# Last token group of a hybrid decoder layer: the eight samples as eight more columns of the first feed-forward product, in halves of 256 tokens

## The chip, the cores and the metric

One core of a Trainium2 chip runs the whole kernel. Its engines work side by side, each through its own list of instructions in order: TensorE (PE in the profile, with its weight loads as PEld), VectorE (DVE), ScalarE (ACT), GpSimd (POOL), and SyncE (SP), which here issues nearly all DMAs. Products land in PSUM, which holds eight banks of 512 float32 words per partition; all else lives in SBUF. The metric is the device time of one execution in microseconds (us), the median of several.

## The reference

One layer of a decoder, applied to a prompt of 2048 tokens and to eight single-token samples with the same weights. Only the second half of the layer matters here:

```python
mixed = concatenate([o_gdn, o_att]) @ w_out           # 1024 -> 1024
x = x + ga1 * mixed
h2 = _rmsnorm(x, g_norm2) * (1.0 + sc2) + sh2         # per-sequence sc2, sh2
gate, up = split(h2 @ w_ffn_in, 2)                    # 1024 -> 2 x 2816
x = x + ga2 * ((silu(gate) * up) @ w_ffn_out)         # 2816 -> 1024
y = _rmsnorm(x, g_final)
```

The prompt and each sample have scales (`sc2`, `ga1` and so on) of their own; the weights are shared.

## The kernel before

The prompt is worked in four groups of 512 tokens (`GT`). `ffn(g)` computes the lines above for group `g`. The first three groups run between attention work; the last one (`samp` is true) also carries the eight samples and runs alone, after everything else is done.

**Split products.** Each float32 product is made of three matmuls in a faster format: both operands are split in a high part (a cast on ACT) and a low part (a subtraction on DVE or POOL), and `mm3` (L199 to L201) issues high x high, high x low and low x high. Every matmul loads its stationary operand of 128 columns and then streams up to 512 columns.

**Weights.** `weights` (L164) brings a tile of 128 x 512 by DMA, casts it on ACT (L182) and subtracts on DVE (L183). In the last group six split tiles are in flight (tags `wi`, and `kT` with `V`), so the cast of a tile waits until TensorE is done with the tile six before it.

**First product.** The 2816 hidden columns go in eleven pairs of 256. A weight tile of a pair holds 256 gate columns and 256 up columns: four stationary blocks `j` = 0 to 3 of 128 (0 and 1 gate, 2 and 3 up). For each of eight `k` (1024 = 8 x 128) and each `j`, `mm3` streams the 512 tokens (`hh`, `hl`) into one PSUM bank; four banks of tag `d` hold the results. Behind a pair, ACT takes tanh of a gate bank (L2115), DVE forms silu(gate) x up (L2116, L2118), ACT casts (L2121) and POOL subtracts (L2122).

**Samples.** Their eight rows are too few to be worth a stream, so they are the stationary operand: high parts in columns 0 to 7 and low parts in columns 32 to 39 of one block of 40, against which the weight tile streams as 512 columns, once for its high and once for its low part (`mm_s`, L215 and L216, into a bank of tag `g`). `fold` adds the two row groups (L222, L223), `gate` forms the activation in rows (L2065 to L2067), and `turned` transposes it back to columns (L2072) for the second product. These side jobs wait in a list (`side`) that `tick` empties behind each weight tile.

**Second product.** After two pairs (or the last one alone), four (two) row blocks of `w_ffn_out` are applied in two halves of 512 output columns; here tokens are stationary, one bank per 128 tokens. Results are scaled by a row (L1876, DVE) and added into `xt` (L1877, POOL). In the last half of all, the tokens' blocks come one by one (`kept`), and `finish` closes each: squares on ACT, `rnorm` (sum on DVE L471, power -0.5 on POOL L472), scaling in two halves on ACT and DVE, and the DMA out.

**Last norm ahead of the feed-forward.** In the second half of `w_out`, the last two `k` of eight are kept back and applied token block by token block; `shut(t)` adds, squares, norms and scales block `t` (L1966 or L1968). Then `hidden_T` transposes all four blocks for one `k` (L500, four transposes), and makes `hh` and `hl` of it (L502 to L504). Six of the eight `k` are transposed while the first pair runs. The samples' own norm and transposes (`turn`, L2023 to L2031) run as side jobs in the first pair.

The order of instructions on an engine follows the order of the code and the Tile framework's scheduling; in this last group nothing else competes.

## Time and profile before

| | |
|---|---|
| median of 3 runs | 3539.82 us (3529.56 to 3540.5) |
| the profiled execution | 3521.95 us, span of its instructions 3520.2 us |
| busy in the span | TensorE 94%, weight loads 73%, VectorE 60%, ScalarE 42%, GpSimd 17% |
| granted TensorE clock, mean | 0.977 |
| chain that ended last | TensorE 72%, DMA 9%, VectorE 8%, waits without a cause shown 4%, ScalarE 4% |
| first matmul of the last group's first pair | at 3061.97 us |
| last matmul of the kernel's second product | at 3501.23 us |

Busy time counts a matmul until its modelled end, so that streams overlap in it: where TensorE is full, what one matmul costs is the distance from its start to the next one's start. Times within a view are us from the span's start. In a row of the timeline stand start, duration, engine, line, operation, output and inputs with their sizes and, in brackets, how long the engine was idle before it and what ended that.

### The profile page before, as it was taken

How to read it: one execution, taken by the hardware profiler on the slowest of the kernel's cores; microseconds unless marked ns; L12 is line 12 of the kernel's file. 1: busy time of each engine (PE TensorE's matmuls, PEld its weight loads, DVE VectorE, ACT ScalarE, POOL GpSimd, SP SyncE). 2: the span in 40 equal slices, each digit the busy share in tenths (PEclk: the TensorE clock that was granted, in tenths of full speed). 3: DMA queues.
4: the chain of work that ended last, by engine and by line, in shares of the span. 5: the costliest groups of instructions: out<-in, count | busy, mean ns of one | idle time of the engine just before them, and what ended most of it. 6: DMA issues, size and time to landing. Idle time of an engine off the chain costs nothing.

```text
span 3520.2 us, 60159 instructions
## 1 busy us (share of the span) xinstructions
PE 3323.2 (94%) x21994; PEld 2584.3 (73%) x21994; DVE 2121.4 (60%) x4502; ACT 1472.9 (42%) x2855; POOL 584.5 (17%) x539
## 2 busy tenths in 40 slices
PE   7899999999998899999989999999899999999997
PEld 5677777777776777777766777777777777677775
DVE  4656545646844767666767656567666654555445
ACT  4333322423433333454565545455554633323223
POOL 1001000100000132212210122222012212222223
PEclk8999999999999999999999999999999999999999
DMA  8765764775785254555463454336433333422221
GB/s 285 270 204 167 246 210 146 225 242 177 239 284 186 92 177 115 157 165 163 148 200 109 121 164 151 90 111 209 131 96 97 101 110 112 162 82 81 81 81 56
DMA packets 421013, 549.60 MB, mean 156 GB/s; under 512 B 50020, under 2 KB 287817, under 8 KB 420698
## 3 DMA queue, kind: packets, MB, share of 16 engines
q1 hardware_dynamic: 420690, 545.62, 49.1%
q8 instruction: 175, 2.87, 0.3%
q14 instruction: 132, 1.08, 0.1%
q10 hardware_dynamic: 16, 0.03, 0.0%
HBM read 441.78 MB, written 122.70 MB: 160 GB/s over the span
## 4 chain that ended last, share of the span: by engine, by line
PE 72%; DMA 9%; DVE 8%; issue 4%; ACT 4%; SPq 2%; POOL 1%; ACTq 0%; DVEq 0%; POOLq 0%
PE d L199 17%; PE d L201 16%; PE d L200 16%; PE s L1740 3%; PE g L1802 3%; PE s L1785 3%; DMA wi<-kept 2%; DMA wr<-in_w_ffn_in_dram 1%; PE g L1814 1%; DVE wi L183 1%; ACT bias L1609 1%; PE g L215 1%; PE g L216 1%; DMA wr<-in_w_out_dram 1%; ACT wi L182 1%
## 5 line engine op out<-in xcount | busy, mean ns | idle before, releaser
L199 PE MATMUL d<-hh,wi 128*128 128x512 f32 x1616 | 687.9, 426 | 21.1 <-DVE th L2116 7.6
L200 PE MATMUL d<-hl,wi 128*128 128x512 f32 x1616 | 639.1, 395 | 3.2 <-DVE hl L504 3.0
L201 PE MATMUL d<-hh,wi 128*128 128x512 f32 x1616 | 638.6, 395 | 0.5 <-DVE wi L183 0.5
L183 DVE TENSOR_TENSOR wi<-wr,wi 128x512 fp32r<-128x512 f32 x525 | 392.0, 747 | 408.1 <-ACT wi L182 403.8
L182 ACT CAST wi<-wr 128x512 fp32r<-128x512 f32 x525 | 324.4, 619 | 693.6 <-PE d L201 397.9
L199 PEld LDWEIGHTS d<-hh,wi 128*128 128x128 f32 x1616 | 308.2, 191 | 104.6 <-issue 11.7
L200 PEld LDWEIGHTS d<-hl,wi 128*128 128x128 f32 x1616 | 308.2, 191 | 74.3 <-issue 10.1
L201 PEld LDWEIGHTS d<-hh,wi 128*128 128x128 f32 x1616 | 307.1, 190 | 69.1 <-DVE wi L183 1.1
L199 PE MATMUL d<-wi,hh 128*128 128x512 f32 x736 | 316.3, 430 | 19.9 <-DMA wi<-kept 10.6
L200 PE MATMUL d<-wi,hh 128*128 128x512 f32 x736 | 291.0, 395 | 1.0 <-DVE wi L183 1.0
L201 PE MATMUL d<-wi,hl 128*128 128x512 f32 x736 | 291.2, 396 | 0.0
L199 PE MATMUL d<-wi,ah 128*128 128x512 f32 x616 | 267.6, 434 | 11.5 <-ACT ah L2121 5.4
L2122 POOL TENSOR_TENSOR al<-ca,ah 128x512 fp32r<-128x512 f32 x88 | 120.3, 1378 | 806.6 <-ACT ah L2121 772.8
L201 PE MATMUL d<-wi,al 128*128 128x512 f32 x616 | 246.1, 400 | 2.4 <-POOL al L2122 2.4
L200 PE MATMUL d<-wi,ah 128*128 128x512 f32 x616 | 245.3, 398 | 0.0
L1749 DVE SCALAR_TENSOR_TENSOR sc<-rl,iw,sc 128x512 f32<-128x512 f32 (+3 forms) x224 | 173.3, 774 | 74.6 <-ACT rl L1742 68.8
L1877 POOL TENSOR_TENSOR xt<-xt,tm 128x512 f32<-128x512 f32 x96 | 136.3, 1434 | 439.1 <-DVE tm L1876 331.1
L1742 ACT ACTIVATE rl<-s 128x512 f32<-128x512 f32 (+3 forms) x288 | 151.3, 542 | 137.6 <-PE s L1740 130.1
L199 PEld LDWEIGHTS d<-wi,hh 128*128 128x128 f32 x736 | 139.8, 190 | 63.5 <-DMA wi<-kept 10.5
L1609 ACT ACTIVATE bias<-sc,sv 128x640 bf16<-128x640 f32 (+11 forms) x120 | 169.8, 1415 | 26.4 <-DVE sv L1611 14.1
L1740 PE MATMUL s<-ik,iqT 128*128 128x512 f32 (+3 forms) x576 | 171.7, 392 | 3.1 <-DVE st L1786 1.6
L201 PEld LDWEIGHTS d<-wi,hl 128*128 128x128 f32 x736 | 139.7, 190 | 31.8 <-issue 0.3
(570 smaller groups left out, 5937.8 us busy)
## 6 DMA issues: line engine op xcount, KB each, us to landing
wi<-kept SPq DMA_DIRECT2D x168, 512.0 KB
wr<-in_w_ffn_in_dram SPq DMA_DIRECT2D x584, 128.0 KB
wr<-in_w_ffn_out_dram SPq DMA_DIRECT2D x148, 256.0 KB
kept<-wi SPq DMA_DIRECT2D x56, 512.0 KB
row<-in_w_ada_dram SPq DMA_DIRECT2D x32, 512.0 KB
wr<-in_w_in_dram SPq DMA_DIRECT2D x56, 256.0 KB
xt<-in_x_prompt_dram SPq DMA_DIRECT2D x7, 2048.0 KB
kT<-kT_d SPq DMA_DIRECT2D x54, 256.0 KB
```

The costliest lines, as they stand in the source:

```text
L182: nc.scalar.copy(hi, wr)
L183: nc.vector.tensor_tensor(lo, wr, hi.bitcast(F32), op=OP.subtract)
L199: self.o(nc.tensor.matmul(out, wh, xh, start=start, stop=False, **kw))
L200: self.o(nc.tensor.matmul(out, wh, xl, start=False, stop=False, **kw))
L201: self.o(nc.tensor.matmul(out, wl, xh, start=False, stop=stop, **kw))
L1609: nc.scalar.activation(c, s, AF.Sign, bias=t, accum_out=cnt)
L1740: self.o(nc.tensor.matmul(ps[:, :w], iq[:, h, :].bitcast(F32R), B["ikT"][c * 2 + a][:, :w].bitcast(F32R), start=a == 0, stop=a == 1))
L1742: nc.scalar.activation(r[:, :w], ps[:, :w], AF.Relu)
L1749: nc.vector.scalar_tensor_tensor(s, r[:, :w], iw, s, op0=OP.mult, op1=OP.add)
L1785: self.o(nc.tensor.matmul(ps[:, :w], qT[:, h, :], kT[:, :w], start=True, stop=True))
L1877: (nc.vector if soon else nc.gpsimd).tensor_tensor(xt, xt, tm, op=OP.add)
L2122: nc.gpsimd.tensor_tensor(al[b], a, ah[b].bitcast(F32), op=OP.subtract)
```

## The change

It touches the last group alone (but for helper lines, so that line numbers grow by 2 ahead of `ffn` and by 14 to 40 in it).

- The eight samples are no longer a stationary operand of the first product. Their normed and transposed values stand as columns 256 to 263 of the second half of `hh` and `hl`, and stream with it. A PSUM bank holds 512 columns, not 520, so the tokens go in halves: 256 of the first half (from tiles of tag `big`, into two banks of tag `s`, which hold gate and up side by side) and 264 of the second (into the four banks of tag `d`). Blocks go in the order 0, 2, 1, 3. `mm_s` and its `fold`, `gate` and `turned` are gone from the first product; in the second they stay.
- The activation behind a pair is made half by half, in twice as many instructions of half the size; two small POOL copies per block put the samples' columns into the stationary block of the second product.
- In the first pair, `k` 0 to 3 run for the first half of the tokens, then for the second half, then `k` 4 to 7 likewise; transposes (`half_T`) come two blocks at a time.
- Three `k` of `w_out` are kept back, not two, and the samples' part of `w_out` is finished ahead of the token blocks. The samples' norm (`turn`) is called behind the second block; it scales on ACT, its transposes stand in the first pair behind `k` = 1.
- The samples' two additions behind each half of `w_out` and `w_ffn_out` move from DVE to POOL.

```diff
@@ -51,6 +51,8 @@
 GONE = -3.0e38
 PAD = -2.0e38
 SEARCH = 10
+KEEP = 3
+HT = GT // 2
...
+    def half_T(self, k, e, xn, to, Amul, Badd):
+
+        nc = self.nc
+        pt = self.ps.tile([128, 512], F32, name="g", tag="g", bufs=2)
+        for t in range(2):
+            self.o(nc.tensor.transpose(pt[:, t * 128:(t + 1) * 128], xn[e * 2 + t][:, k * 128:(k + 1) * 128], self.id))
+        h = self.p.tile([128, 512], F32, name="ca", tag="ca", bufs=2)[:, :HT]
+        nc.vector.tensor_scalar(h, pt[:, :HT], Amul[:, k, 0:1], Badd[:, k, 0:1], op0=OP.mult, op1=OP.add)
+        hi, lo = [x[:, k, 0:HT] for x in to]
+        nc.scalar.copy(hi, h)
+        nc.vector.tensor_tensor(lo, h, hi.bitcast(F32), op=OP.subtract)
...
-                nc.vector.tensor_tensor(t, t, rws[:, cs], op=OP.mult)
-                nc.vector.tensor_tensor(xs[:, cs], xs[:, cs], t, op=OP.add)
+                nc.gpsimd.tensor_tensor(t, t, rws[:, cs], op=OP.mult)
+                nc.gpsimd.tensor_tensor(xs[:, cs], xs[:, cs], t, op=OP.add)
...
+        def turn(ms):
+            xk = q.tile([128, D], F32, name="bias", tag="bias", bufs=2)[:NS]
+            r = self.rnorm(ms[:NS, 4:5], NS)
+            nc.scalar.activation(xk, xs, AF.Copy, scale=r)
+
+            def rest(to):
+                pt = P("g")
+                for k in range(KB):
+                    self.o(nc.tensor.transpose(pt[:, k * NS:(k + 1) * NS], xk[:, k * 128:(k + 1) * 128], self.id[:NS, :NS]))
+                h = s2()[:, :KB * NS].rearrange("p (k n) -> p k n", k=KB)
+                nc.vector.tensor_tensor(h, pt[:, :64].rearrange("p (k n) -> p k n", k=KB), self.A2[:, :, 1:9], op=OP.mult)
+                nc.gpsimd.tensor_tensor(h, h, self.mod[:, 24:32, 1:9], op=OP.add)
+                hi, lo = [x[:, :, HT:HT + NS] for x in to]
+                nc.scalar.copy(hi, h)
+                nc.gpsimd.tensor_tensor(lo, h, hi.bitcast(F32), op=OP.subtract)
+            return rest
...
-                if samp and hf and k >= KB - 2:
+                if samp and hf and k >= KB - KEEP:
                     kept.append((k, wh, wl))
                 else:
                     yield from three(pd, lambda t: oh[:, k, S(t)], lambda t: ol[:, k, S(t)], wh, wl, k, KB - 1)
+            if kept:
+                yield from tick(True)
+                outs(pq, hf)()
+                self.squares(ms[:NS, 4], xs, NS)
             for t in range(4 if kept else 0):
                 for k, wh, wl in kept:
                     self.mm3(pd[t], oh[:, k, S(t)], ol[:, k, S(t)], wh, wl, k == 0, k == KB - 1)
                     yield 3 * MM, 0, bank(t, k, KB - 1)
                 shut(t)
-                if t == 0:
-                    yield from tick()
-                    outs(pq, hf)()
-                    self.squares(ms[:NS, 4], xs, NS)
-            for _ in kept:
-                yield from tick()
+                if t == 1:
+                    turned = turn(ms)
+            if kept:
+                self.done += len(kept) - 1
...
-        yield 0, 4 if samp else 10, dict(act=3, dve=4, need="s")
-
-        def hidden(k):
+        yield 0, 0 if samp else 10, dict(act=3, dve=4, need="s")
+        sides = [(hh, hl)]
+        if samp:
+            sides = [[q.tile([128, KB, HT], F32R, name="big", tag="big", bufs=2) for _ in range(2)], [x[:, :, :HT + NS] for x in (hh, hl)]]
+
+        def hidden(k, e=0):
             if k < KB:
-                self.hidden_T(k, xn, hh, hl, self.A2, B2, "s", 2)
+                if samp:
+                    self.half_T(k, e, xn, sides[e], self.A2, B2)
+                else:
+                    self.hidden_T(k, xn, hh, hl, self.A2, B2, "s", 2)
 
...
-                pq = P("g") if samp else None
-                for k in range(KB):
+                order, areas = range(4), [[x] for x in pd]
+                if samp:
+                    more = [P("s") for _ in range(2)]
+                    order = (0, 2, 1, 3)
+                    areas = [[more[j % 2][:, j // 2 * HT:j // 2 * HT + HT], pd[order[j]][:, :HT + NS]] for j in range(4)]
+
+                def tiles(k):
                     kr = slice(k * 128, (k + 1) * 128)
-                    wh, wl = weights([A["w_ffn_in"][0, kr, f0:f0 + 256], A["w_ffn_in"][0, kr, FF + f0:FF + f0 + 256]])
-                    if samp:
-                        side.append((None, lambda k=k, pq=pq, wh=wh, wl=wl: self.mm_s(pq, box["sx"][:, k, :], wh, wl, k == 0, k == KB - 1), 2 * MM))
-                    for j in range(4):
-                        self.mm3(pd[j], wh[:, S(j)], wl[:, S(j)], hh[:, k, :], hl[:, k, :], k == 0, k == KB - 1)
+                    return weights([A["w_ffn_in"][0, kr, f0:f0 + 256], A["w_ffn_in"][0, kr, FF + f0:FF + f0 + 256]])
+
+                def products(k, j, wh, wl, *parts):
+                    for i in parts:
+                        kw = dict(skip_group_check=True) if samp and not i else {}
+                        self.mm3(areas[j][i], wh[:, S(j)], wl[:, S(j)], sides[i][0][:, k, :], sides[i][1][:, k, :],
+                                 k == 0 and not (samp and not i and j > 1), k == KB - 1, **kw)
+
+                for k0 in (0, KB // 2) if samp and not pr else ():
+                    ks, ws = range(k0, k0 + KB // 2), []
+                    for e in range(2):
+                        for k in ks:
+                            if not e:
+                                ws.append(tiles(k))
+                            for j in order:
+                                products(k, j, *ws[k - k0], e)
+                                yield 1.5 * MM, 0, bank(j, k, KB - 1, act=0.6) if e == (k > 0) else {}
+                            if not e and k == 1:
+                                turned(sides[1])
+                                self.rows_s(rws, 40)
+                            hidden(k + 2, e)
+                            if not e and not k0 and k > 1:
+                                hidden(k - 2, 1)
+                            yield TP, 0
+                            if e:
+                                yield from tick()
+                for k in range(0 if samp and not pr else KB):
+                    wh, wl = tiles(k)
+                    for j in order:
+                        products(k, j, wh, wl, *range(len(sides)))
                         yield 3 * MM, 0, bank(j, k, KB - 1, act=0.6)
...
+                    ah.append(self.m("ah", F32R))
+                    al.append(self.m("al", F32R))
+                    work, c0 = [], 0
+                    for i, (gt, up) in enumerate(zip(areas[j], areas[2 + j])):
+                        n = gt.shape[-1]
+                        th = (self.th("th") if i + 1 == len(sides) else s2())[:, :n]
+                        nc.scalar.activation(th, gt, AF.Tanh, scale=0.5)
+                        nc.vector.scalar_tensor_tensor(th, th, 1.0, gt, op0=OP.add, op1=OP.mult)
+                        work.append((i, th, up))
+                    for i, th, up in work:
+                        n = up.shape[-1]
+                        cs = slice(c0, c0 + n)
+                        c0 += n
+                        a = (p.tile([128, 512], F32, name="ca", tag="ca", bufs=2) if i + 1 == len(sides) else s2())[:, :n]
+                        nc.vector.scalar_tensor_tensor(a, th, 0.5, up, op0=OP.mult, op1=OP.mult)
+                        nc.scalar.copy(ah[b][:, cs], a)
+                        nc.gpsimd.tensor_tensor(al[b][:, cs], a, ah[b][:, cs].bitcast(F32), op=OP.subtract)
+                    if samp:
+                        nc.gpsimd.tensor_copy(ax[:, b, 0:NS], ah[b][:, GT:GT + NS])
+                        nc.gpsimd.tensor_copy(ax[:, b, 32:32 + NS], al[b][:, GT:GT + NS])```

TensorE, one `k` of a pair, last block `j` of a weight tile (`kT` and `V` are its high and low part, `x` the samples). Before:

```order
L199 MATMUL d<-hh,kT 128x512
L200 MATMUL d<-hl,kT 128x512
L201 MATMUL d<-hh,V 128x512
L215 MATMUL g<-kT,x_32151 40x512
L216 MATMUL g<-V,x_32151 40x512
```

The same block in the changed kernel (`big` is the first half of the tokens):

```order
L201 MATMUL s<-big,kT 128x256
L202 MATMUL s<-big,kT 128x256
L203 MATMUL s<-big,V 128x256
L201 MATMUL d<-hh,kT 128x264
L202 MATMUL d<-hl,kT 128x264
L203 MATMUL d<-hh,V 128x264
```

Three matmuls became six of half the length, with a load each, and the two that streamed the weights past the samples are gone.

ScalarE, between the second half of `w_out` and the first pair (`junk,msq<-xt` are the squares of a token block, `sc` of the samples; `rnz` is a norm; `wi` and `kT` are weight casts). Before:

```order
L182 CAST wi<-wr 128x512
L182 CAST kT<-rl 128x512
L464 ACTIVATE junk,msq<-sc 8x512
L464 ACTIVATE junk,msq<-xt 128x512 x3
L1966 ACTIVATE sc<-xt,rnz_32021 128x1024
L1966 ACTIVATE bias<-xt,rnz_32053 128x1024
L503 CAST hh<-ca 128x512 x3
```

In the changed kernel:

```order
L466 ACTIVATE junk,msq<-xt 128x512 x2
L184 CAST kT<-PT 128x512
L184 CAST wi<-wr 128x512
L1997 ACTIVATE sc<-xt,rnz_32015 128x1024
L184 CAST kT<-rl 128x512
L1977 ACTIVATE bias<-sc,rnz_32021 8x1024
L466 ACTIVATE junk,msq<-xt 128x512
L517 CAST big<-ca 128x256
L466 ACTIVATE junk,msq<-xt 128x512
L517 CAST big<-ca 128x256
L1997 ACTIVATE bias<-xt,rnz_32059 128x1024
```

The first cast of a transposed half (L517) now stands ahead of the squares and the scaling of the fourth block; three weight casts and the samples' scaling stand ahead of it.

GpSimd, the end of the kernel (`xt<-xt,row` multiplies a token block by the final norm's gains, `s` and `sc` belong to the samples). Before:

```order
L2159 TENSOR_TENSOR xt<-xt,row 128x512 x4
L472 TENSOR_TENSOR rnz_35463<-rny_35462,mhalf 128x1
L472 TENSOR_TENSOR rnz_35482<-rny_35481,mhalf 128x1
L472 TENSOR_TENSOR rnz_35512<-rny_35511,mhalf 8x1
L472 TENSOR_TENSOR rnz_35529<-rny_35528,mhalf 128x1
L472 TENSOR_TENSOR rnz_35548<-rny_35547,mhalf 128x1
```

In the changed kernel:

```order
L2198 TENSOR_TENSOR xt<-xt,row 128x512 x2
L1947 TENSOR_TENSOR s_36490<-s_36490,sc 8x512
L2198 TENSOR_TENSOR xt<-xt,row 128x512 x2
L1947 TENSOR_TENSOR s_36499<-s_36499,sc 8x512
L474 TENSOR_TENSOR rnz_36464<-rny_36463,mhalf 128x1
L474 TENSOR_TENSOR rnz_36483<-rny_36482,mhalf 128x1
L1948 TENSOR_TENSOR sc<-sc,s_36490 8x512
L1948 TENSOR_TENSOR sc<-sc,s_36499 8x512
L474 TENSOR_TENSOR rnz_36509<-rny_36508,mhalf 8x1
L474 TENSOR_TENSOR rnz_36526<-rny_36525,mhalf 128x1
L474 TENSOR_TENSOR rnz_36545<-rny_36544,mhalf 128x1
```

The samples' four operations now stand on POOL ahead of the last three powers, where DVE had them.

More of the change, by code (lines that the diff above doesn't have):

```diff
@@ L2015, in ffn @@
         hidden(1)
[L2016 to L2036 removed]
+        yield TP, 0 if samp else 2.5, dict(dve=1.5, use="s", need="d")
         gf = []
@@ L2096, in ffn @@
                 pd = D4()
-                pq = P("g") if samp else None
-                for k in range(KB):
-                    kr = slice(k * 128, (k + 1) * 128)
-                    wh, wl = weights([A["w_ffn_in"][0, kr, f0:f0 + 256], A["w_ffn_in"][0, kr, FF + f0:FF + f0 + 256]])
-                    if samp:
-                        side.append((None, lambda k=k, pq=pq, wh=wh, wl=wl: self.mm_s(pq, box["sx"][:, k, :], wh, wl, k == 0, k == KB - 1), 2 * MM))
-                    for j in range(4):
-                        self.mm3(pd[j], wh[:, S(j)], wl[:, S(j)], hh[:, k, :], hl[:, k, :], k == 0, k == KB - 1)
+                order, areas = range(4), [[x] for x in pd]
```

46 lines of the change are left out of this document (1 added, 45 removed).

## The prediction

> **What bounds the kernel now.** I read the busy time by stretches first. In the last group, from the second pair on, TensorE never stands idle. The columns are the window, its length, busy time and instructions of PE, PEld, DVE, ACT and POOL, the granted clock, the DMA share and GB/s:
>
> ```profile
> 3101.00:3485.50 384.50, 384.50 (x1673) 294.19 (x1671) 191.60 (x263) 108.06 (x193) 87.75 (x62) 1.00 0.26 77
> 3050.00:3060.00 10.00, 3.05 (x13) 1.84 (x11) 7.98 (x18) 6.41 (x12) 3.58 (x5) 0.85 0.33 105
> 3060.00:3070.00 10.00, 9.29 (x31) 6.96 (x32) 4.14 (x6) 1.86 (x3) 0.00 (x0) 0.64 0.00 0
> 3485.60:3488.40 2.80, 0.96 (x4) 0.32 (x3) 2.16 (x4) 1.94 (x4) 1.38 (x2) 1.00 0.00 0
> 3501.80:3520.20 18.40, 0.00 (x0) 0.00 (x0) 10.09 (x19) 5.73 (x12) 5.71 (x7) 0.56 0.35 122
> ```
>
> In the first row PE is busy for the whole 384.50 us at clock 1.00 and issues 1673 matmuls: 384.50 / 1673 = 0.2298 us for one. DVE is busy for half of that, ACT and POOL for less, DMA for a quarter: there, time is the number of PE's columns and nothing else. Three places are otherwise: the last norm (rows two and three: PE 3.05 of 10 us, then a clock of 0.64), the passage from the last pair to its second product (row four), and the tail without matmuls (row five). I take each alone.
>
> **A. The samples' matmuls go.** By groups of equal form and by the timeline (start, duration, engine, line, operation, output and inputs):
>
> ```profile
> L215 PE MATMUL g<-wi,x 128*40 128x512 f32 x74 | 29.3, 396 | 0.4 <-ACT sc L1856 0.4
> L215 PE MATMUL g<-kT,x 128*40 128x512 f32 x74 | 29.3, 395 | 0.0
> L216 PE MATMUL g<-V,x 128*40 128x512 f32 x74 | 29.2, 395 | 0.0
> L216 PE MATMUL g<-wi,x 128*40 128x512 f32 x74 | 29.1, 393 | 0.0
> 3334.52 0.39 PE L201 MATMUL d<-hh,V 128*128 128x512 f32 x1
> 3335.06 0.42 PE L215 MATMUL g<-wi,x 128*40 128x512 f32 x1
> ```
>
> Of these 4 x 74 = 296, the first product has 8 `k` x 2 x 11 pairs = 176; `w_out` (32) and `w_ffn_out` (88) keep theirs. At one pitch each, since PE is full: 176 x 0.2298 = **-40.4**. The two transposes of the gate (L2072) stand between the last two rows: 3334.52 + 0.23 = 3334.75 to 3335.06, so 0.31 a pair, 11 x 0.31 = **-3.4**. The others can follow: in some 11% less time DVE's share of 191.60 / 384.50 = 0.50 and the DMA share of 0.26 grow to 0.56 and 0.29, and the weights' DMAs keep their order and number.
>
> **B. Streams of 512 become 256 and 264.** 8 x 4 x 3 x 11 = 1056 matmuls become 2112, with 1056 more loads.
>
> ```profile
> 3332.00 0.39 PE L199 MATMUL d<-hh,kT 128*128 128x512 f32 x1
> 3332.23 0.39 PE L200 MATMUL d<-hl,kT 128*128 128x512 f32 x1
> 3332.00 0.19 PEld L200 LDWEIGHTS d<-hl,kT 128*128 128x128 f32 x1
> 1808.03 0.40 PE L1740 MATMUL s<-ik,iqT 128*128 128x256 f32 x2
> 1808.26 0.40 PE L199 MATMUL d<-wi,hh 128*128 128x512 f32 x1
> 1408.07 1.09 PEld L1411 LDWEIGHTS g<-s,s 128*128 128x128 f32 x8
> ```
>
> The load for the second matmul starts with the first (3332.00) and is over before the second starts at 3332.23: it costs nothing beside 512 columns. Beside 256 the nearest row is L1740: two streams of 256 columns take 1808.26 - 1808.03 = 0.23, so 0.115 each, half of a whole one. The other bound is the pace of loads with nearly nothing to stream: eight take 1.09, less the 0.19 of the last that is (1.09 - 0.19) / 7 = 0.13 each. I take 0.117 for 256 columns, near the first row, which is the same kind of stream, and 0.120 for 264: 1056 x (0.237 - 0.2298) = **+7.6**. By 0.115 and 0.1186 for 264 it is +4, by 0.13 and 0.134 +36.
>
> The Trainium skill's page "TensorE: Matmul & The Clock Gate" says in Part 3, "The mechanism", that a load overlaps matmuls in flight only when its row group differs (though the same section lets one run ahead into a background buffer). All loads here take all rows, so by it each added load would stand in series, and the sum would be that of rival 1. The trace speaks against it: the load at 3332.00 lies beside a matmul of all 128 rows.
>
> **C. The last norm.** The timeline, with the idle time ahead and its releaser in brackets:
>
> ```profile
> 3051.59 0.39 PE L201 MATMUL d<-kT,hl 128*128 128x512 f32 x1
> 3052.01 0.62 ACT L182 CAST kT<-rl 128x512 fp32r<-128x512 f32 x1
> 3052.58 0.33 PE L500 MATMUL s<-cf,sc 128*128 128x128 f32 x1 [0.60 <-DVE sc L1968]
> 3056.22 0.63 ACT L464 ACTIVATE junk<-xt 128x512 f32<-128x512 f32 x1 [0.78 <-DVE rny L471]
> 3056.76 0.19 ACT L464 ACTIVATION_READ_ACCUMULATOR junk<-xt 128x1 f32 x1
> 3056.92 1.15 ACT L1966 ACTIVATE sc<-xt,rnz 128x1024 f32<-128x1024 f32 x1
> 3058.13 0.47 PE L500 MATMUL s<-cf,sc 128*128 128x128 f32 x1 [5.23 <-ACT sc L1966]
> 3059.94 0.48 PE L500 MATMUL s<-cf,bias 128*128 128x128 f32 x1 [1.12 <-ACT bias L1966]
> 3061.97 0.79 PE L199 MATMUL d<-hh,wi 128*128 128x512 f32 x1 [0.70 <-ACT hh L503]
> 3067.20 0.40 PE L201 MATMUL d<-hh,wi 128*128 128x512 f32 x1
> 2476.76 2.08 PE L1802 MATMUL g<-PT,V 128*128 128x256 f32 x4 [2.21 <-ACT PT L1817]
> 2476.80:2478.80 2.00, 2.00 (x4) 1.13 (x4) 1.95 (x7) 2.00 (x6) 0.35 (x1) 0.50 0.90 267
> ```
>
> `w_out` ends at 3051.59 + 0.23 = 3051.82, the first `k` of the first pair at 3067.20 + 0.23 = 3067.43. These 15.6 us hold 12 matmuls (12 x 0.23 = 2.76) and eight transposes (some 0.9, at 0.11 each, just under the 0.13 of B's last row), so 11.96 are lost: 10.15 until the first matmul at 3061.97, the rest to a slow clock behind the gap. The first matmul waits for the fourth block's norm (`bias`, L1966), which ends last.
>
> Afterwards it needs two blocks only, and these are closed while PE still applies the kept `k` to the other two. What is late next is ACT, whose queue now holds in front of the first `hi` cast three weight casts, the scaling of block 1 and of the samples, and squares. Counted from `w_out`'s end by these rows: a cast that is nearly over (0.1), scaling 1.15, a cast 0.62, scaling of the samples 1.15, squares 0.63 + 0.19, the `hi` cast 0.40 (group below), the low part on DVE 0.41: 4.7, less 0.5 of transposes that lie in it, so some **4.2** of idle PE instead of 9.3. Behind it there may be a slow clock: a gap of 2.21 us ahead of 2476.76 was followed by a clock of 0.50. One slow stretch like the present one costs 11.96 - 10.15 = 1.8. Together 6.0 lost of now 11.96: **-6.0**. Ends: nothing, where ACT's queue takes as long as the present chain, and -12, where nothing at all is lost.
>
> The same page, in "Why this matters for your kernels", asks for no idle gaps on PE above some 3 us, as one such window brings the slow clock back. By it a gap that came out just under 3 us would leave the clock alone, and the sum would be lower by the 1.8. The row at 2476.76 disagrees, at 2.21.
>
> **D. The activation in halves.** By groups, the prices of work on 256 columns:
>
> ```profile
> L1224 DVE TENSOR_TENSOR AT<-g,dec 128x256 f32<-128x256 f32 x32 | 13.2, 413 | 0.0
> L1830 ACT COPY PT<-g 128x256 f32<-128x256 f32 x24 | 8.9, 370 | 11.5 <-PE g L1828 11.4
> L1835 ACT CAST PT<-oT 128x256 fp32r<-128x256 f32 x24 | 9.7, 403 | 11.7 <-DVE oT L1833 11.7
> L1836 POOL TENSOR_TENSOR oT<-oT,PT 128x256 fp32r<-128x256 f32 x24 | 20.4, 850 | 273.5 <-ACT PT L1835 185.4 <-issue 88.0
> ```
>
> The next pair's first matmul overwrites the `s` bank of block 0, so it waits for that block's last DVE step, and its 13th matmul for block 1's. The blocks go 0, 2, 1, 3, each 6 x 0.118 = 0.71 in the last `k`. Block 0's gate ends 2.13 ahead of the pair's end. Two tanh (0.4 each, the second behind the up half's stream at -1.78) and four DVE steps of 0.41 from -1.7 on bring DVE to -0.05, and block 1's four steps to +1.6, where PE wants its bank at 1.42. So 0.2 to 0.4 of wait, five times (the other six pair ends go to the second product): 5 x 0.4 = **+2**, from 0 to +7, should a weight subtraction on DVE (0.747) stand in between. Transposes in twos instead of fours make eight groups more, each with up to 0.09 besides its streams (the 0.31 of two in A, less 2 x 0.11): **+0.5**.
>
> **E. The end.** By the timeline and a group:
>
> ```profile
> 3485.42 0.39 PE L216 MATMUL g<-V,x 128*40 128x512 f32 x1
> 3488.38 0.50 PE L201 MATMUL d<-wi,al 128*128 128x512 f32 x1 [0.66 <-POOL al L2122]
> 3497.58 6.34 POOL L2159 TENSOR_TENSOR xt<-xt,row 128x512 f32<-128x512 f32 x4
> L1399 POOL TENSOR_TENSOR s<-s,s 128x512 f32<-128x512 f32 x8 | 8.4, 1049 | 52.0 <-PE g L1394 49.9 <-issue 2.0
> 3511.20 0.93 POOL L472 TENSOR_TENSOR rnz<-rny,mhalf 128x1 f32<-128x1 f32 x1 [1.00 <-DVE sc L2081]
> 3512.17 0.75 DVE L2053 SCALAR_TENSOR_TENSOR xt<-xt,rnz,row 128x512 f32<-128x512 f32 x1 [0.45 <-POOL rnz L472]
> ```
>
> Between the last pair (3485.42) and its second product (3488.38) PE waits for POOL's `al`, two instructions of 1.4. In halves the first is ready earlier, but POOL makes four: **-0.4**. In the tail the samples' four operations go from DVE to POOL, ahead of the powers that the last blocks need (3511.20, then 3512.17). Each costs 1.05 (L1399) to 1.6 (6.34 / 4). Most stand where POOL is free or waits; I take **+1**, from -2, DVE's relief alone, to +3, two of them in the chain.
>
> **Sum.** -40.4 - 3.4 + 7.6 - 6.0 + 2 + 0.5 - 0.4 + 1 = **-39**. The profiled execution took 3521.95 (span 3520.2 and 1.75 around it), 0.5% less than the median of the runs, 3539.82. 3521.95 - 39 = 3483, a ratio of 0.9889; on the median that is **3500 us**.
>
> **Rivals.**
>
> 1. **Loads become the bound (slower).** If an added load isn't hidden beside 256 columns and each matmul takes a load's 0.19, a pair of halves costs 0.38: 1056 x (0.38 - 0.2298) = +159 in place of +7.6, net +112: about 3652. It decides from a pitch of (0.2298 + 46.7 / 1056) / 2 = 0.137 on. For it: the loads' records of 0.19, longer than 0.115. Against: L1740's two at 0.115 with a load each, and eight loads at 0.13 apiece. Chance 0.04. Within the forecast's own mechanism, at 0.13, the sum is -11: 0.3%, about what a measurement of this kernel can tell from no change, is 10.6 us. I give that end 0.04.
> 2. **The pair's end becomes the bound.** Twice as many DVE and ACT steps with the weight casts and subtractions among them delay each of eleven pair ends by two DVE steps and a subtraction, 2 x 0.41 + 0.75 = 1.6, less the 0.2 counted: 11 x 1.4 = +15, so 3516. For it: the bank of block 1 is late by 0.2 already. Against: DVE is busy for 191.6 of 384.5. Chance 0.08.
> 3. **The last norm isn't shorter.** The change doesn't do there what it says: ACT's queue of casts and scalings only replaces the wait for block 4, and the -6 goes: 3507. For it: 4.7 us of ACT work ahead of the first cast, each with its own wait for POOL's power. Against: the present chain has four blocks in series. Chance 0.11.
>
> **How the numbers follow.** The forecast has 0.77 (0.04 of it at the loads' end), the rivals 0.04, 0.08 and 0.11. Faster by over 0.3% are the forecast without that end and rivals 2 and 3: 0.73 + 0.08 + 0.11 = 0.92; within 0.3%: 0.04; slower: 0.04. The range: all good ends at once (-3.6, -6, -2, -3) give 3486, and 7 less, since single runs spread over 11 (3529.56 to 3540.5), is 3479. Upward it takes in rivals 2 and 3, with about the same 7 on rival 2: 3522. Left out are rival 1 and the loads' end.
>
> **What would show it.** Right: 1056 matmuls of 256 columns and 1056 of 264 with starts 0.117 and 0.120 apart at clock 1.00; L215 and L216 with 120 in all in place of 296; a gap of some 4 us between `w_out` and the first half product, where 10 stood; less than 0.4 idle at a pair's end. Wrong: a pitch above 0.13, PE waiting for DVE at every pair's end, a first pair that waits for ACT as long as before, or a tail in which POOL's additions precede the last power by over 3 us.

## The result, and the profile after

The changed kernel took 3499.54 us (median of 4 runs, 3494.76 to 3502.24), the kernel before 3536.75 (4 runs, 3529.56 to 3540.5): a ratio of 0.9896, 95% interval 0.9874 to 0.9918. That is 37.2 us less, 1.04%; 3500 had been forecast. The profiled execution has a span of 3499.8 us.

The two profiles can't be compared by their spans alone. The code ahead of the last group's `w_out` is the same in both, but that part ended at 2998.14 us in the profile of before and at 3013.04 in this one, 15 us later. So the last group is read by itself, by starts of matmuls: from `w_out`'s first one to the first of the first pair, from there to the last of the second product, and the tail to the span's end (the page gives spans to 0.1 us, so the tails are no finer).

| stage of the last group (us) | before | after | difference |
|---|---|---|---|
| `w_out` and last norm | 63.83 | 57.25 | -6.58 |
| of it idle or transposes, behind `w_out`'s last matmul | 10.15 | 3.70 | -6.45 |
| first and second products | 439.27 | 407.10 | -32.17 |
| tail | 18.96 | 22.39 | +3.43 |
| all | 522.06 | 486.75 | -35.31 |

By stretches (window, length, busy time of PE, PEld, DVE, ACT and POOL, clock, DMA share, GB/s), after:

```profile
3070.20:3076.80 6.60, 6.17 (x26) 5.70 (x26) 3.16 (x9) 2.55 (x6) 1.53 (x2) 0.50 0.41 133
3140.00:3445.00 305.00, 304.96 (x2078) 276.38 (x2077) 131.06 (x212) 88.11 (x175) 118.44 (x126) 1.00 0.29 88
3462.90:3463.90 1.00, 0.29 (x4) 0.08 (x2) 0.86 (x4) 0.93 (x4) 0.57 (x1) 1.00 0.00 0
3477.80:3499.80 22.00, 0.12 (x2) 0.01 (x2) 9.15 (x15) 5.72 (x14) 12.75 (x12) 0.62 0.28 102
```

In the second row PE is still full, DVE's share has fallen, and POOL's has grown to 118 of 305. The first row is the slow start of the first pair, the third the passage from the last pair to its second product, the last one the tail: there POOL is now the busiest engine.

The samples' groups and one step of a pair, by groups and by the timeline, after:

```profile
L217 PE MATMUL g<-wi,x 128*40 128x512 f32 x30 | 11.8, 394 | 0.2 <-ACT sc L1870 0.2
L217 PE MATMUL g<-kT,x 128*40 128x512 f32 x30 | 11.8, 395 | 0.0
L218 PE MATMUL g<-V,x 128*40 128x512 f32 x30 | 11.9, 395 | 0.0
L218 PE MATMUL g<-wi,x 128*40 128x512 f32 x30 | 11.9, 396 | 0.0
...
3330.15 0.28 PE L203 MATMUL s<-big,V 128*128 128x256 f32 x1
3330.27 0.28 PE L201 MATMUL d<-hh,kT 128*128 128x264 f32 x1
3330.39 0.28 PE L202 MATMUL d<-hl,kT 128*128 128x264 f32 x1
3330.51 0.28 PE L203 MATMUL d<-hh,V 128*128 128x264 f32 x1
3330.63 0.28 PE L201 MATMUL s<-big,wi 128*128 128x256 f32 x1
```

4 x 30 = 120 are left of 296, as the change says, and a half product starts 0.12 us behind the one before. From one second product to the next there were 78.20 us before (3120.67 to 3198.87) and are 71.99 now (3126.04 to 3198.03): 6.21 less for two pairs.

The last norm, in the timeline:

```profile
3066.37 0.39 PE L203 MATMUL d<-kT,hl 128*128 128x512 f32 x1
...
3068.20 1.14 ACT L1977 ACTIVATE bias<-sc,rnz 8x1024 f32<-8x1024 f32 x1
3068.58 0.53 DVE L515 TENSOR_SCALAR ca<-g,A,mod 128x256 f32<-128x256 f32 x1
3069.25 0.61 ACT L466 ACTIVATE junk<-xt 128x512 f32<-128x512 f32 x1
3069.86 0.39 ACT L517 CAST big<-ca 128x256 fp32r<-128x256 f32 x1
3070.30 0.58 PE L201 MATMUL s<-big,wi 128*128 128x256 f32 x1 [1.92 <-ACT big L517]
3071.21 0.58 PE L202 MATMUL s<-big,wi 128*128 128x256 f32 x1 [0.33 <-DVE big L518]
3071.59 0.42 PE L203 MATMUL s<-big,wi 128*128 128x256 f32 x1
3071.81 0.42 PE L201 MATMUL s<-big,wi 128*128 128x256 f32 x1
```

The first cast's input is done at 3068.58 + 0.53 = 3069.11, but ACT is at the samples' scaling and then at squares: the cast starts at 3069.86. Behind it a second wait shows, 0.91 from the first to the second matmul, for DVE's low part. Then half products start 0.22 apart where 0.12 is normal.

The tail:

```profile
3477.40 0.40 PE L203 MATMUL d<-kT,al 128*128 128x512 f32 x1
3479.22 3.45 POOL L2198 TENSOR_TENSOR xt<-xt,row 128x512 f32<-128x512 f32 x2
3480.51 1.05 DVE L1891 TENSOR_TENSOR xt<-xt,ca 128x512 f32<-128x512 f32 x1
3482.64 1.25 POOL L1947 TENSOR_TENSOR s<-s,sc 8x512 f32<-8x512 f32 x1
3483.86 1.06 POOL L474 TENSOR_TENSOR rnz<-rny,mhalf 128x1 f32<-128x1 f32 x2
3484.89 3.08 POOL L1948 TENSOR_TENSOR sc<-sc,s 8x512 f32<-8x512 f32 x2
3486.34 0.63 ACT L466 ACTIVATE junk<-sc 8x512 f32<-8x512 f32 x1 [0.57 <-POOL sc L1948]
3488.01 0.63 ACT L466 ACTIVATE junk<-sc 8x512 f32<-8x512 f32 x1 [0.95 <-POOL sc L1948]
3488.76 0.63 ACT L466 ACTIVATE junk<-xt 128x512 f32<-128x512 f32 x1
3491.30 0.72 ACT L2070 ACTIVATE xt<-xt,rnz 128x512 f32<-128x512 f32 x1 [1.07 <-POOL rnz L474]
```

DVE has the last token block added up at 3480.51 + 1.05 = 3481.56. Its squares run after 3488.76, since they stand on ACT behind the samples' squares, which wait for POOL's last additions, which wait for POOL's products with the final gains.

### The profile page after: what moved, and what is told of

Its sections match the earlier page's. It is cut to its first block, busy times and chain, and to the rows that moved or that the text cites. A ratio compares the mean times of both kernels' runs of the same rounds, so it can differ in the third digit from the quotient of the medians.

```text
span 3499.8 us, 61968 instructions
## 1 busy us (share of the span) xinstructions
PE 3300.3 (94%) x22852; PEld 2623.9 (75%) x22852; DVE 2076.9 (59%) x4488; ACT 1470.0 (42%) x2875; POOL 640.8 (18%) x633
## 3 DMA queue, kind: packets, MB, share of 16 engines
q14 instruction: 131, 1.07, 0.1%
## 4 chain that ended last, share of the span: by engine, by line
PE 71%; DMA 9%; DVE 9%; issue 5%; ACT 4%; SPq 1%; POOL 1%; ACTq 0%; DVEq 0%; POOLq 0%
PE d L201 16%; PE d L203 15%; PE d L202 15%; PE s L1754 3%; PE g L1816 3%; PE s L1799 3%; DMA wr<-in_w_ffn_in_dram 2%; DMA wi<-kept 1%; DVE wi L185 1%; PE g L1828 1%; PE s L202 1%; PE s L201 1%; PE s L203 1%; ACT bias L1623 1%; ACT wi L184 1%
## 5 line engine op out<-in xcount | busy, mean ns | idle before, releaser
L201 PE MATMUL d<-hh,wi 128*128 128x512 f32 (+1 forms) x1616 | 669.8, 414 | 20.2 <-DVE th L2153 7.6
L185 DVE TENSOR_TENSOR wi<-wr,wi 128x512 fp32r<-128x512 f32 x525 | 391.9, 747 | 396.9 <-ACT wi L184 392.4
L202 PE MATMUL d<-hl,wi 128*128 128x512 f32 (+1 forms) x1616 | 620.7, 384 | 4.7 <-DVE hl L506 4.4
L203 PE MATMUL d<-hh,wi 128*128 128x512 f32 (+1 forms) x1616 | 620.8, 384 | 0.0
L184 ACT CAST wi<-wr 128x512 fp32r<-128x512 f32 x525 | 324.6, 619 | 680.9 <-PE d L203 427.1
L201 PEld LDWEIGHTS d<-hh,wi 128*128 128x128 f32 x1616 | 308.3, 191 | 94.0 <-issue 11.7
L202 PEld LDWEIGHTS d<-hl,wi 128*128 128x128 f32 x1616 | 308.8, 191 | 68.4 <-issue 10.1
L203 PEld LDWEIGHTS d<-hh,wi 128*128 128x128 f32 x1616 | 307.6, 190 | 62.1 <-DVE wi L185 0.8
L201 PE MATMUL d<-wi,hh 128*128 128x512 f32 x736 | 317.6, 432 | 17.5 <-DMA wi<-kept 7.7
L202 PE MATMUL d<-wi,hh 128*128 128x512 f32 x736 | 291.9, 397 | 1.0 <-DVE wi L185 1.0
L203 PE MATMUL d<-wi,hl 128*128 128x512 f32 x736 | 292.4, 397 | 0.0
L201 PE MATMUL d<-wi,ah 128*128 128x512 f32 x616 | 267.9, 435 | 10.7 <-ACT ah L2161 5.0
L203 PE MATMUL d<-wi,al 128*128 128x512 f32 x616 | 246.9, 401 | 2.4 <-POOL al L2162 2.4
L202 PE MATMUL d<-wi,ah 128*128 128x512 f32 x616 | 245.9, 399 | 0.0
L2162 POOL TENSOR_TENSOR al<-ca,ah 128x512 fp32r<-128x512 f32 (+1 forms) x88 | 107.6, 1228 | 732.1 <-ACT ah L2161 698.3
L1891 POOL TENSOR_TENSOR xt<-xt,tm 128x512 f32<-128x512 f32 x96 | 136.9, 1441 | 426.3 <-DVE tm L1890 341.0
L201 PEld LDWEIGHTS d<-wi,hh 128*128 128x128 f32 x736 | 140.3, 191 | 61.1 <-DMA wi<-kept 11.3
L203 PEld LDWEIGHTS d<-wi,hl 128*128 128x128 f32 x736 | 140.4, 191 | 32.2 <-issue 0.3
```

What stands on the lines that cost most here:

```text
L184: nc.scalar.copy(hi, wr)
L185: nc.vector.tensor_tensor(lo, wr, hi.bitcast(F32), op=OP.subtract)
L201: self.o(nc.tensor.matmul(out, wh, xh, start=start, stop=False, **kw))
L202: self.o(nc.tensor.matmul(out, wh, xl, start=False, stop=False, **kw))
L203: self.o(nc.tensor.matmul(out, wl, xh, start=False, stop=stop, **kw))
L1891: (nc.vector if soon else nc.gpsimd).tensor_tensor(xt, xt, tm, op=OP.add)
```

## The experiments

All but three are the changed kernel with an edit. The stages of each, from its trace, in us:

| run | `w_out`, norm | of it idle | products | tail | last group |
|---|---|---|---|---|---|
| before | 63.83 | 10.15 | 439.27 | 18.96 | 522.06 |
| e5_halves (of before) | 63.96 | 10.15 | 447.60 | 18.40 | 529.96 |
| e6_quarters (of before) | 63.71 | 10.14 | 673.52 | 18.62 | 755.85 |
| e7_no_mms (of before) | 63.67 | 10.15 | 402.33 | 18.35 | 484.35 |
| after | 57.25 | 3.70 | 407.10 | 22.39 | 486.75 |
| e1_dve | 59.37 | 5.06 | 406.76 | 18.99 | 485.12 |
| e2_samples_first | 57.27 | 3.70 | 406.13 | 24.04 | 487.44 |
| e3_keep2 | 61.35 | 7.26 | 406.44 | 22.03 | 489.83 |
| e4_keep4 | 56.88 | 3.28 | 406.72 | 22.10 | 485.70 |
| e8_xk_pool | 57.01 | 3.00 | 406.74 | 22.15 | 485.90 |
| e9_tail | 57.26 | 3.70 | 406.02 | 20.68 | 483.96 |
| e10_norm | 57.85 | 4.22 | 407.03 | 22.16 | 487.04 |
| e11_both | 57.88 | 4.22 | 406.72 | 19.90 | 484.49 |
| e12_last_dve | 57.28 | 3.28 | 406.66 | 19.05 | 482.99 |

Stages that an edit doesn't touch agree within 0.7 us, and the idle part where the code ahead of it is the same within 0.01; the times of whole runs scatter by ten and more. One exception: the first pair of e2_samples_first and e9_tail, the same code as in the changed kernel, is 1.0 shorter (last section), and that is all that their products' stage gained. So differences above one can be read here.

### The price of the products

**e7_no_mms**, of the kernel before:

```diff
-                    if samp:
+                    if samp and k == 1:
-                        side.append((None, lambda ...: self.mm_s(..., k == 0, k == KB - 1), 2 * MM))
+                        side.append((None, lambda ...: self.mm_s(..., True, True), 2 * MM))
```

> The kernel before, with the samples' matmuls of the first product left out for seven of the eight k (154 of 176), so that the samples' part of the feed-forward is left out for these. Theory, TensorE is full and each was worth its whole pitch: 154 x 0.2298 = -35.4, the product stage goes from 439.26 to 403.9 within 1.5. Rival, they partly stood where TensorE would have waited for the activation at a pair's end anyway: -25 to -31, and waits for DVE or ACT at the pair ends.

Measured: 402.33, so -36.94, or 0.240 for each of 154. The theory holds, 0.1 past the edge of its range: each was worth its pitch of 0.2298 and a trifle more. By this the 176 of the change are worth 42.2.

**e5_halves** and **e6_quarters**, of the kernel before (2 or 4 for `N`):

```diff
-                        self.mm3(pd[j], wh[:, S(j)], wl[:, S(j)], hh[:, k, :], hl[:, k, :], k == 0, k == KB - 1)
+                        w_ = GT // N if samp else GT
+                        for c in range(0, GT, w_):
+                            self.mm3(pd[j][:, c:c + w_], wh[:, S(j)], wl[:, S(j)], hh[:, k, c:c + w_], hl[:, k, c:c + w_], ...)
```

> The kernel before, whose first product of the last group streams 256 + 256 tokens, each with a load of its own, in place of 512; the samples stay as they were. Its product stage (first matmul of the first pair to the last of the second product) was 439.26 us. Theory, a short stream costs 0.117 as in the changed kernel: 1056 x (0.234 - 0.2298) = +4.4, so 442 to 446. Rival, the loads set the pace of short streams by more than the starts in the changed kernel show, 0.13 and above: +32 and more, 471 upward.

> The kernel before, whose first product of the last group streams four times 128 tokens, each with a load of its own. Theory, a load takes about 0.11 of PE's time when there is next to nothing to stream (eight loads with one column each start 0.111 apart in the profile of before), and 256 columns at 0.115 lie just above it: a stream of 128 then costs 0.11, not 0.0575, and the stage grows by 1056 x (4 x 0.111 - 0.2298) = +226 to 665. Rival, loads are hidden at any length: 1056 x (4 x 0.0585 - 0.2298) = +4, so 443 to 448.

Halves: 447.60, so +8.33, 1.6 above the expected range and far from the rival: a pair of halves costs 0.2298 + 8.33 / 1056 = 0.2377, each 0.119. Quarters: 673.52, +234: a stream of 128 columns costs (0.2298 + 234.25 / 1056) / 4 = 0.113. The timeline of the run with quarters, loads beside matmuls:

```profile
3330.51 0.27 PE L199 MATMUL d<-hh,kT 128*128 128x128 f32 x1
3330.56 0.19 PEld L200 LDWEIGHTS d<-hl,kT 128*128 128x128 f32 x1
3330.62 0.28 PE L200 MATMUL d<-hl,kT 128*128 128x128 f32 x1
3330.67 0.19 PEld L201 LDWEIGHTS d<-hh,V 128*128 128x128 f32 x1
```

Loads are recorded with 0.19 but start 0.11 apart: the records overlap, and 0.11 is the pace. So a load is hidden beside 256 columns (0.119) with a margin of some 5%, and at 128 columns it is the bound. A least time of 0.11 for any matmul is not the cause: in the profile of before two matmuls of 128 columns whose loads start 0.23 apart (L1740, 1322.37 and 1322.60) start 0.06 apart themselves (1322.60 and 1322.66). The row-group rule on the Trainium skill's page "TensorE: Matmul & The Clock Gate" (Part 3, "The mechanism") would have had every added load in series, since all use all rows; the halves disagree, at 0.119 a stream. Its section on LDWEIGHTS gives a load its columns divided by 1.2 in ns, 107 for 128, and the quarters agree, at 0.113 us.

### The last norm

**e3_keep2** and **e4_keep4**:

```diff
-KEEP = 3
+KEEP = 2        # or 4
```

> The changed kernel with two k of w_out kept back instead of three. Theory, the idle time ahead of the first pair is the chain of norm of the first two token blocks, which the matmuls of the other two cover: one k less covers 2 x 3 x 0.23 = 1.4 us less, so the stage up to the first pair grows from 57.26 to 58.6 us. Rival, ACT's queue alone (weight casts, the samples' scaling, squares) sets it: 57.3 within 0.3. The rest of the last group stays within 0.7.

> The changed kernel with four k of w_out kept back instead of three. Theory, as for two: 1.4 us more of the norm is covered and the stage up to the first pair falls from 57.26 to 55.9 us, and the first pair's slow clock becomes shorter or vanishes (0 to 2.7 less in the product stage of 407.10). Rival, ACT's queue sets it: 57.3 within 0.3 and the product stage as before.

With two the stage grew by 4.10, neither the theory's 1.4 nor the rival's nothing. The timeline of that run points to a third cause, which no run takes out:

```profile
3053.79 1.00 DVE L1891 TENSOR_TENSOR xt<-xt,tm 128x512 f32<-128x512 f32 x1
3054.32 1.62 POOL L1948 TENSOR_TENSOR sc<-sc,s 8x512 f32<-8x512 f32 x1
3055.97 0.63 ACT L466 ACTIVATE junk<-sc 8x512 f32<-8x512 f32 x1 [3.80 <-POOL sc L1948]
3057.11 0.62 ACT L466 ACTIVATE junk<-xt 128x512 f32<-128x512 f32 x1
```

The first block is added up at 3054.79, but ACT stands idle in front of the samples' squares until POOL is done, and the block's squares come at 3057.11. With three `k` kept the samples' squares run at 3062.45, 4 us ahead of `w_out`'s end. With four the stage fell by 0.37 only, 0.1 below the range of the rival, ACT's queue, and far from the theory's 1.4; the idle part fell by 0.42.

**e8_xk_pool**:

```diff
-            nc.scalar.activation(xk, xs, AF.Copy, scale=r)
+            nc.gpsimd.tensor_scalar(xk, xs, r, None, op0=OP.mult)
```

> The changed kernel, with the samples' scaling by their norm (1.14 us on ACT, ahead of the first cast of a transposed half) on POOL. Theory, ACT's queue holds the first cast back, by 0.75 us (its input was ready at 3069.1, it starts at 3069.86): the stage up to the first pair falls from 57.26 by 0.5 to 0.8. Rival, the chain of the second block's norm sets it: 57.3 within 0.2.

The idle time fell by 0.70, as the theory had it, but `w_out` itself took 53.78 between its first and last matmul in place of 53.32 (scatter: with four `k` kept it takes 53.37 and, with the same code, 53.77 in e12_last_dve), so that the stage fell by 0.24, between the two. So ACT's queue held the first matmul back by these 0.70, but it is not what holds the pair back. In the timeline of that run:

```profile
3066.00 0.39 PE L201 MATMUL s<-big,wi 128*128 128x256 f32 x1 [1.22 <-ACT big L517]
3066.51 0.68 DVE L185 TENSOR_TENSOR V<-rl,kT 128x512 fp32r<-128x512 f32 x1
3067.18 0.41 DVE L518 TENSOR_TENSOR big<-ca,big 128x256 fp32r<-128x256 f32 x1
3067.64 0.39 PE L202 MATMUL s<-big,wi 128*128 128x256 f32 x1 [1.26 <-DVE big L518]
```

The second matmul needs DVE's low part, which stands behind a weight subtraction. It starts 4.64 behind `w_out`'s end (3063.00), where it starts 4.62 behind it in the changed kernel and 4.81 with four `k` kept. A shorter queue on ACT moves the wait from the first matmul to the second: by these three timelines DVE's queue sets the time of the second, though no run frees it.

**e10_norm**:

```diff
-KEEP = 3
+KEEP = 4
-        nc.scalar.copy(hi, h)
+        (nc.vector.tensor_copy if k < 2 and not e else nc.scalar.copy)(hi, h)
-                if t == 1:
+                if t == 3:
                     turned = turn(ms)
```

> The changed kernel with four k of w_out kept back, with the high parts of the first two transposed halves made on DVE in place of ACT, and the samples' scaling called behind the fourth block in place of the second. Theory, ACT's queue, not the norm, sets the idle time ahead of the first pair once three k are kept: without it in the way the idle time of 3.70 us (w_out's last matmul over to the first product) falls to 2.0 to 2.6. Rival, the second block's norm and its transposes set it: 3.2 or more, as with four k kept back alone (3.28). The slow clock behind the gap stays, as the gap of 2.21 us in the profile of before was followed by a clock of 0.50, so the products' stage stays within 1 of 407.10.

The theory fell: 4.22 of idle time in place of 3.70, within the rival's range, though the rows below show DVE's queue and not the norm in the way. DVE, in the timeline of that run:

```profile
3061.05 0.53 DVE L515 TENSOR_SCALAR ca<-g,A,mod 128x256 f32<-128x256 f32 x1
3061.57 0.68 DVE L1891 TENSOR_TENSOR xt<-xt,ca 128x512 f32<-128x512 f32 x1
3062.17 0.68 DVE L185 TENSOR_TENSOR wi<-wr,wi 128x512 fp32r<-128x512 f32 x1
3062.77 0.68 DVE L185 TENSOR_TENSOR V<-rl,kT 128x512 fp32r<-128x512 f32 x1
3063.37 0.28 DVE L517 CAST big<-ca 128x256 fp32r<-128x256 f32 x1
```

The cast's input is there at 3061.58. On DVE it stands behind an addition and two weight subtractions and starts 1.8 later, where on ACT it had waited 0.75. By these rows it is the place in a queue that costs, on either engine; a version that puts the cast and the low part first on DVE was not tried.

### The tail

**e1_dve**, **e2_samples_first**:

```diff
-                nc.gpsimd.tensor_tensor(t, t, rws[:, cs], op=OP.mult)            # e1
-                nc.gpsimd.tensor_tensor(xs[:, cs], xs[:, cs], t, op=OP.add)
+                nc.vector.tensor_tensor(t, t, rws[:, cs], op=OP.mult)
+                nc.vector.tensor_tensor(xs[:, cs], xs[:, cs], t, op=OP.add)
```

```diff
+                if kept:                                                         # e2
+                    yield from tick(True)
+                    outs(pq, hf)()
+                    self.squares(ms[:NS, 4], xs, NS)
+                    sums()
                 for t in range(4 if kept else 0):
...
-                    if t == 1:
-                        yield from tick(True)
-                        outs(pq, hf)()
-                        self.squares(ms[:NS, 4], xs, NS)
-                        sums()
```

> The changed kernel, with the samples' multiplications and additions behind each half of w_out and w_ffn_out on DVE again. The last group is read in three stages: from w_out's first matmul to the first one of the first pair (57.26 us in the changed kernel), from there to the last matmul of all (407.10), and the tail behind it to the end of the span (22.40, where the kernel before had 18.97). Theory, POOL's four operations stand ahead of the last powers and hold ACT's squares of the last blocks back: the tail falls by 3.4 to about 19.0, the other two stages stay within 0.5. Rival, the tail is longer because the last product ends in another rhythm: it stays at 22.4 within 0.5.

> The changed kernel, with the samples' last product, sum, squares and output ahead of the four token blocks of the last half, where they stood behind the second block. Theory, the tail of 22.40 us is ACT's squares of the last two blocks waiting behind the samples' squares: with those done under the blocks' matmuls, what is left behind the last matmul is 0.5 to its end, 0.7 + 0.7 on DVE, 0.8 of squares, 1.3 for sum and power, 0.8 of scaling and some 6 for the DMA: 11 to 14 us, so 8 to 11 less, and the stage of the products unchanged within 1. Rival, POOL's four products with the final gains (1.7 each) hold the powers back whatever the samples do: 18 to 22.

With the operations on DVE the tail is 18.99, as the theory had it, and the whole +3.4 is gone. But `w_out` and the norm lost 2.12, 1.36 of it idle ahead of the first pair: there POOL was the right place. With the samples first the tail grew to 24.04, worse than both theories. In the timeline of that run:

```profile
3477.27 2.47 POOL L2198 TENSOR_TENSOR xt<-xt,row 128x512 f32<-128x512 f32 x2
3479.71 2.47 POOL L1948 TENSOR_TENSOR sc<-sc,s 8x512 f32<-8x512 f32 x2
3480.99 0.63 ACT L466 ACTIVATE junk<-sc 8x512 f32<-8x512 f32 x1 [9.69 <-POOL sc L1948]
```

POOL reaches the samples' additions only at 3479.71, 6.3 us behind the last product (3473.36), and now all token blocks' squares stand behind them on ACT, idle for 9.69. Earlier in the program was not earlier in time: POOL's queue was the bound.

**e9_tail**: as e2_samples_first, and

```diff
-                    after(0, 0, outs(pq, hf))
+                    after(0, 0, outs(pq, hf, nc.vector if last else nc.gpsimd))
-                    gated_add(pd[t], row[:, cs], xt[:, t, cs], last and hf, t)
+                    gated_add(pd[t], row[:, cs], xt[:, t, cs], last and (hf or samp), t)
```

with `outs` on DVE in the last half too.

> The changed kernel with the samples' last product, sum and squares ahead of the token blocks, and with POOL freed in the end: the samples' four operations there are on DVE, and the four additions behind the first half of the last second product too; in w_out they stay on POOL. Theory, the second run above showed that POOL's queue sets the tail (ACT stood idle for 9.69 us until POOL's last addition for the samples): without it the tail of 22.40 falls to 14 to 17, below the 18.97 of the kernel before, and the products' stage stays within 1 of 407.10. Rival, DVE, which has ten operations of 0.67 more around the end, becomes the bound in POOL's place: 18 or more.

20.68: less than the changed kernel, but the rival holds. DVE in that run:

```profile
3476.07 0.67 DVE L1948 TENSOR_TENSOR sc<-sc,s 8x512 f32<-8x512 f32 x1
...
3477.94 0.67 DVE L1948 TENSOR_TENSOR sc<-sc,s 8x512 f32<-8x512 f32 x1
3478.54 1.27 DVE L1891 TENSOR_TENSOR xt<-xt,ca 128x512 f32<-128x512 f32 x2
3478.98 0.63 ACT L466 ACTIVATE junk<-sc 8x512 f32<-8x512 f32 x1 [1.43 <-DVE sc L1948]
```

DVE has the last block added up at 3479.81, 7.0 behind the last product (3472.83); in the changed kernel it was 4.2 behind.

### Put together

**e11_both** has the edits of e9_tail and e10_norm. **e12_last_dve** has `KEEP = 4`, the samples where the change put them, and DVE for their operations in the last second product alone:

```diff
-                        outs(pq, hf)()
+                        outs(pq, hf, nc.vector)()
-                    after(0, 0, outs(pq, hf))
+                    after(0, 0, outs(pq, hf, nc.vector if last else nc.gpsimd))
```

> The changed kernel with the edits of the two runs above together. Theory, they add up: the last group from w_out's first matmul to the end of the span falls from 486.75 to 477 to 480 us, 7 to 10 less, and the time is 1.2 to 1.4% below that of the kernel before (the changed kernel had 1.04%). Rival, they meet on DVE, which then holds up the first pair or the tail: 483 or more.

> The changed kernel with four k of w_out kept back and with the samples' four operations on DVE in the last second product alone (on POOL in w_out and in the other second products). Theory, the two effects of the first run come apart: in w_out POOL is the right place (the first run, with DVE there too, lost 2.1 us ahead of the first pair), in the end DVE is. So the stage up to the first pair is 56.9 within 0.3 as with four k kept, the products 407.1 within 0.7, the tail 19.0 within 0.5, the last group 482.5 to 483.5, some 3.7 less than in the changed kernel, and the ratio to the kernel before about 0.988 to 0.989, which the interval cannot tell from the changed kernel's. Rival, the order on DVE in the tail depends on what ran ahead, and the tail is 21 or more.

The first: 484.49, 2.3 less than the changed kernel and not the 7 to 10 expected, since both of its parts had fallen short (-2.8 and +0.3; they do add up, though the number lies in the rival's range); ratio to the kernel before 0.9887 (0.9868 to 0.9907). The second: tail 19.05, products 406.66, last group 482.99, 3.8 less than the changed kernel, as expected; its first stage came to 57.28 (`w_out` took 53.77 again), 0.1 above the expected range. Ratio 0.9907 (0.9886 to 0.9928), where 0.988 to 0.989 was expected. By stages it is the best of all; by time neither can be told from the changed kernel, as the intervals overlap. Both intervals lie below 1.

## Why the prediction was right

Time and direction came out: 3500 against 3499.54, and the samples' matmuls carry it. But the sum for the last group was -39.1, and -35.3 was measured there. That the medians differ by 37.2 and the forecast was met to half a microsecond is luck: the forecast went from a median of 3539.82 for the kernel before, which came out 3.1 lower with one more run. Step by step:

- **A** (-40.4 - 3.4): right. e7_no_mms gives 42.2 for 176 where 40.4 was taken, a little too small. The transposes' -3.4 was not measured by itself.
- **B** (+7.6), with **D**'s +2: right in size. Two pairs are 6.21 shorter; 32 matmuls at 0.235 (the same run's second products stand 71.62 apart in place of 78.20, for 28 left out) and two gates at 0.31 would give 8.14. So 1.93 is lost on 192 products, 0.0100 each, 10.6 on all 1056, where 9.6 was forecast (7.6, and 2 for the pairs' ends; the 0.5 for transposes falls into the first pair). e5_halves says what of it: 8.3 is the splitting alone, which leaves 2.3 for the eight columns and the waits at a pair's end. The forecast had split it otherwise.
- **C** (-6.0): the gap fell by 6.45, more than forecast (4.2, and 0.5 of transposes, were to be left, and 3.70 was), but the first pair gave 2.8 back. From its first matmul to its second product it took 58.70 before, 7.0 more than a later two pairs (51.69); now 55.74, 9.85 more than 45.89. With the stage of `w_out` and the norm, -6.58, that is -3.7. The step that failed is "one slow stretch like the present one", priced at 1.8. By the prediction's own rows the present one cost 2.7: the 10.15 still holds the 0.9 of transposes that the 11.96 leaves out (15.61 - 10.15 - 2.76). In the changed kernel the 24 half products and two transposes up to 3076.85 took 6.55, where 3.0 is normal: 3.5 lost, to half the clock and to 0.7 of wait for DVE's low part, which wasn't priced. 1.0 of it is a second slow stretch, which the same code has in one run and not in another (last section). What makes up the rest of the 2.8 was not measured by itself.
- **E**: the passage to the last second product gained 0.9, not 0.4 (15.58 from the last matmul's end there to the last product before, 14.39 now, less 0.31 for the transposes of A). The prediction read 3488.38 as that product's start; its first matmul stands at 3487.00, behind a wait of 1.19 for ACT's `ah`, and `al` cost another 0.66. Now the two waits are 0.71 and 0.35. The **tail** was mis-sized: "+1, from -2 to +3", and +3.43 was measured, beyond the end. The mechanism was named (the samples' operations ahead of the powers); "most stand where POOL is free or waits" is what failed. POOL is busy there without a break until 3484.89 + 3.08 = 3487.97, and what waits behind that is ACT's squares of the last two blocks; their powers come only after these. e1_dve shows that all of it comes from there.
- **Rival 1** is out: the pitch is 0.119, not 0.137. **Rival 2** is out: less than 2.3 in all is left for pair ends, and the idle time of PE that the rows show sums up to 0.04 in 305 us (second row by stretches; waits shorter than a modelled end are not seen). **Rival 3** is half true: ACT's queue of casts and scalings did take the place of the old wait, at 3.70 in place of 10.15, and DVE's queue stands right behind it, at 4.62.

Left open: whether the part ahead of the last group is unchanged in time. The profiles of the four kernels with the code of before reach `w_out` at 2997.95 to 3001.75, the ten with the changed code at 2998.98 to 3013.04, 7.5 later on the mean, most of it between 950 and 1150 us of the span. Nothing there differs in the program's order. By the profiles a part of the gain is lost there; the medians (37.2, 36.5 and 33.5 less for the changed kernel, e11_both and e12_last_dve, whose last groups are 35.3, 37.6 and 39.1 shorter) allow anything from none to some 6 us. The 25 timed runs of the kernel before spread from 3516.85 to 3540.5, and no run here separates it.

## What to carry to other kernels

A few rows that share a stationary operand with a long stream are cheapest as extra columns of that stream, also where a bank's size forces the stream in two: two halves with a load each and eight columns more cost 4% more than the whole (0.0100 on 0.2298), the separate matmuls had cost 17% (42.2 on 1056 x 0.2298); below some 256 columns the load's own 0.11 takes over (an estimate: 0.113 is what 252 columns take at 0.2298 for 512). Before work is moved to an idle engine, look at that engine in every stage: POOL was free beside `w_out` (2.1 us gained) and the bound at the end (3.4 lost). An instruction that is called earlier in the program, but waits for a busy engine, holds up all that stands behind it in its own queue. And a shorter wait for the first operand is no gain while the second one comes as late as before: read the time up to a later point.
